# Grouping the small attention products of a hybrid decoder step, and loading the decode cache two steps at a time

## The chip, the core and the metric

The kernel runs on one core of one Trainium2 chip. The metric is the device time of one launch in microseconds, lower is better. The five engines that the text speaks of are PE (TensorE, matrix products; PEld are its weight loads), DVE (VectorE), ACT (ScalarE), POOL (GpSimd, which issues the indirect gathers) and SP (SyncE, which issues nearly all other transfers in one queue, in order).

## The reference, cut to what matters

One inference step of one decoder layer, for 1024 prompt tokens and for 8 decode sequences of 4 new tokens each:

```
proj = x @ w_in                                   # q,k,v of attention; q,k,v of GLA; gates
for g, (window, dil) in enumerate(((128,1),(512,4),(2048,16))):
    o_g, lse_g = dilated windowed softmax attention, 8 heads of 64, T5 bias
o_a  = sum_g softmax_g(lse_g) * o_g
o_b  = GLA recurrence (4 heads, 128 x 256 state), RMS norm, silu gate
x    = LN(ALPHA*x + (sigmoid(ga)*(o_a@wa) + sigmoid(gb)*(o_b@wb)) @ w_out)
x    = LN(ALPHA*x + PEER(x))                      # 8 heads x 16 of 16384 experts per token
```

In decode attention a new token at step s of its sequence (s = 0 to 3) reads, in groups 1 and 2, the cached keys at positions s, s+dil, s+2*dil and so on. The four steps of a sequence read four different key tiles of 128 positions, and four different value tiles. In group 0 (dilation 1) the four steps share one tile.

PEER picks experts per token and needs the rows of two 16384 x 1024 tables: for 544 columns of expert numbers (four blocks of 128 prompt tokens, and the decode tokens) the kernel gathers rows by index; for the other 512 tokens it multiplies by the whole tables ("dense").

## The kernel before, in words

The work is written as a program of tiles, and a scheduler puts the instructions of each engine into one fixed order before the launch: it follows the tiles' dependences, a priority (mostly the order in which the program text issues the work) and the time at which it expects an instruction's inputs and its tile's buffer to be free. On the chip every engine works through its own order without overtaking, and SP through its queue of transfers. A change of a few lines can therefore move instructions everywhere.

A tile's buffer comes from a ring named by a tag: `wst` (3 buffers, weight tiles as they land), `tq` (6 buffers of 2 KB per partition), `gr` (4 buffers of 4 KB per partition, made for the gathered rows), `pb` (3 PSUM banks), `ps` (4 PSUM banks).

The stages, on the time axis of the trace:

- `phase_a(0)`, from the start to about 918 us: projections of prompt tokens 0 to 511 and the 32 decode tokens (every weight tile lands in `wst`, is split into two parts by ACT, L143, and by DVE, L158, and is used by three products per output tile, L185 to L187), with three lanes that feed smaller work in between: prompt attention (`attend`), the GLA heads, and the decode lane (`sample_attention`, then `sample_gla`). It ends with the output projection and a layer norm, whose result is transposed (L815) for what follows.
- `query(0)`: the expert queries, first for token block 0 alone (32 weight tiles from `wq`, three products each), then for blocks 1 to 3. Its scores give the first top-k, and with it the first gather (L1233 on POOL, about 1065 us).
- `phase_a(1)` and its queries, for tokens 512 to 1023, to about 2300 us, with the gathers of the first blocks beside it (POOL issues, DVE multiplies and accumulates: L1239, L1272).
- `peer_dense`, to the end, with the last gathers beside it.

The small products of the change:

- `attend`, L356: for two query blocks p2 (and, where there are keys before them, two key blocks c) and the two heads r of a pair, one product of 64 rows. Head r uses rows 64r to 64r+63 of the array and writes to PSUM tile `p_[r]`.
- `sample_attention`, L1075 (keys): per sequence and group, for four head pairs hp and four steps s, a product that writes 32 output partitions 32s to 32s+31, that is, it uses 32 of the 128 columns of the array. Step s needs key tile `kts[s]`, one 256 KB transfer (L1068) into a `tq` buffer.
- `sample_attention`, L1128 (values): per sequence and group, four products of 32 columns, one per step, on value tiles loaded by L1125 into `tq`. L1120 is group 0's value product, L1132 what follows a sequence's value products.
- `sample_gla`, L1182 and L1187: the decode GLA's small products, on states that L1180 loads and L1191 stores.

One of these float32 products shows as two instructions in the trace (x2), so sixteen key products show as x32.

Of the kernel before, what the change touches and what calls it, by code (L numbers as in the profile page):

```python
# [3 lines left out]

# [1 line left out]

# [15 lines left out]
P = 128  # L22
# [59 lines left out]
def tile_hybrid_step(ctx, tc, I, O, dbg=None):  # L82
# [239 lines left out]
    def attend(b, g, hp, q, k, vP, ot, stat):  # L322

        bias = tb([P, 2, 256])
        nc.sync.dma_start(bias, biasd[g][:, 2 * hp:2 * hp + 2])
        np_ = 0 if b == 0 else 1 if g == 0 else 4
        if np_:
            pk, pv = tb([P, 4, P]), tb([P, 4, P])
            nc.sync.dma_start(pk[:, :np_], kprev[g][:, hp, :np_ * P].rearrange("d (p i) -> d p i", i=P))
            nc.sync.dma_start(pv[:, :np_], vprev[g][:, :np_, hp * P:(hp + 1) * P])  # L330

        def keys(p, c):
            if c:
                return k[:, p * P:(p + 1) * P]
            if g == 0 and p > 0:
                return k[:, (p - 1) * P:p * P]
            return pk[:, p] if np_ else None

        def values(p, c):
            if c:  # L340
                return vP[:, p, hp * P:(hp + 1) * P]
            if g == 0 and p > 0:
                return vP[:, p - 1, hp * P:(hp + 1) * P]
            return pv[:, p]

        po = pb()
        for pp in range(2):
            p_ = [pb([P, 2, 256]) for _ in range(2)]
            j0 = []
            for p2 in range(2):  # L350
                p = 2 * pp + p2
                j0.append(0 if keys(p, 0) is not None else P)
                for c in range(j0[p2] // P, 2):
                    for r in range(2):
                        rows = slice(64 * r, 64 * r + 64)
                        nc.tensor.matmul(p_[r][:, p2, c * P:(c + 1) * P], q[rows, p * P:(p + 1) * P], keys(p, c)[rows], start=True, stop=True)  # L356
            s2 = []
            parts = [(0, 2)] if j0[0] == j0[1] else [(0, 1), (1, 2)]
            for r in range(2):
                h = 2 * hp + r  # L360
                s_ = tb([P, 2, 256])
                s2.append(s_)
                for a, e in parts:
                    j = j0[a]
                    if F_TTR:
                        for p2 in range(a, e):
                            V.tensor_tensor_reduce(s_[:, p2, j:], p_[r][:, p2, j:], bias[:, r, j:], 1.0, -3e38, ALU.add, ALU.max, stat[:, 2 * pp + p2, h:h + 1])
                    else:
                        V.tensor_add(s_[:, a:e, j:], p_[r][:, a:e, j:], bias[:, r, None, j:].to_broadcast([P, e - a, 256 - j]))
                        V.reduce_max(stat[:, 2 * pp + a:2 * pp + e, h], s_[:, a:e, j:], axis=AX.X, negate=True)  # L370
                if F_TTR:
                    V.tensor_scalar(stat[:, 2 * pp:2 * pp + 2, h], stat[:, 2 * pp:2 * pp + 2, h], -1.0, None, ALU.mult)
                for p2 in range(2):
                    p, j = 2 * pp + p2, j0[p2]
                    nc.scalar.activation(s_[:, p2, j:], s_[:, p2, j:], AF.Exp, bias=stat[:, p, h:h + 1], accum_out=stat[:, p, 32 + h:33 + h])
            yield
            for p2 in range(2):
                p, c0 = 2 * pp + p2, j0[p2] // P
                t_ = pb([P, 2, 2, P])
                for r in range(2):  # L380
                    for c in range(c0, 2):
                        nc.tensor.transpose(t_[:, r, c], s2[r][:, p2, c * P:(c + 1) * P], ident)
                pt = tb([P, 2, 2, P])
                copy_any(pt[:, :, c0:], t_[:, :, c0:])
                for c in range(c0, 2):
                    v_ = values(p, c)
                    for r in range(2):
                        nc.tensor.matmul(po[r * 64:r * 64 + 64, p * P:(p + 1) * P], v_[:, r * 64:(r + 1) * 64], pt[:, r, c],
                                         start=c == c0, stop=c == 1)
                if p2 == 0:  # L390
                    yield

        cp = copy_act if F_OT and busy[0] else V.tensor_copy
        if g == 0:
            cp(ot[:, hp, :T], po)
        else:
            cp(ot[:, hp, :T].rearrange("d (i r) -> d r i", r=4), po.rearrange("d (r i) -> d r i", r=4))
# [639 lines left out]
        out.extend((f_(ef[0]), f_(ef[1]), ei, f_(gate)))  # L1037

    def sample_attention():
        for hf in range(2):  # L1040
            st = sb([P, 16], "s_st", 2)
            pr = tq([P, 3, 160])
            for g in range(3):
# [18 lines left out]
                for b4 in range(4):  # L1062
                    yield
                    b = hf * 4 + b4
                    kts = []
                    for s in range(1 if g == 0 else 4):
                        kt = tq([P, 4, P])
                        nc.sync.dma_start(kt, I["kc0"][b] if g == 0 else I[f"kc{g}"][b, s])  # L1068
                        kts.append(kt)
                    for hp in range(4):  # L1070
                        if g == 0:
                            nc.tensor.matmul(p_[:, b4], qf[:, hp], kts[0][:, hp], start=hp == 0, stop=hp == 3)
                            continue
                        for s in range(4):
                            nc.tensor.matmul(p_[32 * s:32 * s + 32, b4], qf[:, hp, 32 * s:32 * s + 32], kts[s][:, hp], start=hp == 0, stop=hp == 3)  # L1075
                w_ = pr[:, g]
                V.tensor_copy(w_, pn)
                for b4 in range(4):
# [35 lines left out]
            for b4 in range(4):  # L1114
                yield
                b = hf * 4 + b4
                p_ = pb()
                vt = tq([P, 512])
                nc.sync.dma_start(vt, I["cache1"][b, :, 1])
                nc.tensor.matmul(p_, tT[:, 0], vt, start=True, stop=False)  # L1120
                for g in (1, 2):
                    vts = []
                    for s in range(4):
                        vt = tq([P, 512])
                        nc.sync.dma_start(vt, I[f"cache{g + 1}"][b].rearrange("(i r) c d -> r i c d", r=DIL[g])[s, :, 1])  # L1125
                        vts.append(vt)
                    for s in range(4):
                        nc.tensor.matmul(p_[32 * s:32 * s + 32], tT[:, g, 32 * s:32 * s + 32], vts[s], start=False, stop=g == 2)  # L1128
                om = tq([P, 512])
                V.tensor_mul(om, p_, hm)  # L1130
                for hp in range(4):
                    nc.tensor.matmul(po[:, hp, 4 * b4:4 * b4 + 4], om[:, hp * P:(hp + 1) * P], sel[:, b4], start=False, stop=b4 == 3 and hp == 3)  # L1132
# [573 lines left out]
```

## Time and profile before

| what | us |
|---|---|
| three timed runs: median (lowest to highest) | 4177.53 (4170.21 to 4186.6) |
| the profiled execution: its time | 4168.93 |
| its span | 4167.2 |
| PE busy | 3739.9 (90%) |
| DVE busy | 3147.9 (76%) |
| POOL busy | 1345.5 (32%) |

The profiled execution is 8.6 us under the median of the timed runs. A sum made from the trace is a difference against 4168.93, and is carried over to the median as it is. Busy PE time overlaps from one matmul to the next (their ends are modelled), so the cost of a product is read from the start of one instruction to the start of the next.

### The profile page before, as it was taken

The numbers are of one execution on the slowest core, as the hardware profiler recorded it, in microseconds if no ns is written. First come the engines' busy times: TensorE is split into PE (matmuls) and PEld (weight loads), VectorE is DVE, ScalarE is ACT, GpSimd is POOL, SyncE is SP. The second block draws the span as 40 slices with busy tenths as digits, with TensorE's granted clock in tenths as the row PEclk, the third lists the DMA queues.
The fourth block names the chain that finished last, engine by engine and source line by source line (L and its number), as shares of the span: only waits on it lengthen the run. The fifth ranks groups of instructions, "written<-read, shape, count | busy, mean of one in ns | idle before, by whom it ended". The sixth has DMA issues, their size and how long they took to land.

```text
span 4167.2 us, 55732 instructions
## 1 busy us (share of the span) xinstructions
PE 3739.9 (90%) x18338; PEld 2890.6 (69%) x18338; DVE 3147.9 (76%) x7279; ACT 1444.7 (35%) x2958; POOL 1345.5 (32%) x1163
## 2 busy tenths in 40 slices
PE   8999999999897589999879866788999999999996
PEld 7888666665686478756757544677777777777775
DVE  2334433547999888788989998897888888888878
ACT  3334322324543354523225344332222233223323
POOL 0000000000245334354444322444444444444443
PEclk9999899999898689889889998999999999999997
DMA  8666465788688779778988756877998899999996
GB/s 276 199 215 201 164 201 184 262 272 277 200 310 299 226 260 327 255 243 304 317 300 283 222 199 241 274 249 269 312 311 310 309 318 311 318 318 320 312 320 248
DMA packets 455160, 1118.18 MB, mean 268 GB/s; under 512 B 48484, under 2 KB 133748, under 8 KB 444486
## 3 DMA queue, kind: packets, MB, share of 16 engines
q0 software_dynamic: 156672, 570.49, 39.8%
q1 hardware_dynamic: 298198, 544.13, 39.1%
q8 instruction: 144, 2.36, 0.2%
q14 instruction: 146, 1.20, 0.1%
HBM read 1043.94 MB, written 158.37 MB: 289 GB/s over the span
## 4 chain that ended last, share of the span: by engine, by line
PE 42%; DMA 20%; DVE 17%; issue 13%; POOL 5%; ACT 3%; SPq 0%; POOLq 0%; DVEq 0%; ACTq 0%
PE ps L185 9%; PE ps L186 9%; PE ps L187 9%; DMA gr<-pv,tkei 5%; DMA pg<-Gd 4%; POOL gr L1233 4%; DMA gr<-pu,tkei 3%; DVE gr L1239 3%; DMA wst<-pv 2%; DVE acc L1272 2%; DMA wst<-uT 2%; DVE wl L158 2%; PE pc L1312 2%; POOL gr L1254 2%; DVE tb L1309 1%
## 5 line engine op out<-in xcount | busy, mean ns | idle before, releaser
L1254 POOL DMA_INDIRECT gr<-pv,tkei x544 | 675.2, 1241 | 910.2 <-DVE acc L1272 567.3
L1233 POOL DMA_INDIRECT gr<-pu,tkei x544 | 651.1, 1197 | 951.3 <-DVE gr L1239 543.5
L185 PE MATMUL ps<-pg,wh 128*128 128x512 f32 (+3 forms) x2488 | 896.7, 362 | 65.7 <-ACT wh L143 43.5
L186 PE MATMUL ps<-pg,wl 128*128 128x512 f32 (+3 forms) x2488 | 896.0, 360 | 8.8 <-DVE wl L158 8.6
L187 PE MATMUL ps<-pg,wh 128*128 128x512 f32 (+3 forms) x2488 | 892.5, 360 | 0.0
L143 ACT ACTIVATE wh<-wst 128x512 fp32r<-128x512 f32 x740 | 462.2, 628 | 1148.7 <-DMA wst<-uT 347.7
L158 DVE TENSOR_TENSOR wl<-wst,wh 128x512 fp32r<-128x512 f32 x740 | 502.5, 683 | 346.1 <-ACT wh L143 317.2
L1239 DVE SCALAR_TENSOR_TENSOR gr<-gr,x1g 128x1024 f32<-128x1024 f32 x544 | 660.4, 1220 | 121.5 <-DMA gr<-pu,tkei 119.8
L1272 DVE SCALAR_TENSOR_TENSOR acc<-gr,act,acc 128x1024 f32<-128x1024 f32 x512 | 654.9, 1279 | 70.8 <-DMA gr<-pv,tkei 67.4
L185 PEld LDWEIGHTS ps<-pg,wh 128*128 128x128 f32 (+1 forms) x2488 | 472.2, 190 | 162.7 <-ACT wh L143 49.6
L186 PEld LDWEIGHTS ps<-pg,wl 128*128 128x128 f32 (+1 forms) x2488 | 472.9, 190 | 91.1 <-DVE wl L158 13.3
L187 PEld LDWEIGHTS ps<-pg,wh 128*128 128x128 f32 (+1 forms) x2488 | 472.5, 190 | 77.1 <-issue 10.7
L185 PE MATMUL ps<-wh,pg 128*128 128x512 f32 x832 | 342.2, 418 | 33.2 <-ACT wh L143 20.3
L186 PE MATMUL ps<-wh,pg 128*128 128x512 f32 x832 | 341.6, 411 | 3.7 <-DVE pg L158 3.7
L187 PE MATMUL ps<-wl,pg 128*128 128x512 f32 x832 | 323.5, 415 | 4.0 <-DVE wl L158 3.6
L143 ACT ACTIVATE pg<-wst 128x512 fp32r<-128x512 f32 x256 | 160.0, 630 | 448.0 <-DMA wst<-pv 428.8
L185 PEld LDWEIGHTS ps<-wh,pg 128*128 128x128 f32 x832 | 177.6, 214 | 90.3 <-ACT wh L143 26.7
L1046 POOL MEMSET tq<- 128x512 f32 x6 | 3.2, 526 | 661.7 <-issue 287.2
L187 PEld LDWEIGHTS ps<-wl,pg 128*128 128x128 f32 x832 | 174.9, 213 | 51.8 <-issue 10.8
L185 PE MATMUL ps<-tq,pg 128*128 128x512 f32 x512 | 203.4, 400 | 7.9 <-ACT t L1356 7.8
L186 PEld LDWEIGHTS ps<-wh,pg 128*128 128x128 f32 x832 | 177.4, 213 | 44.1 <-issue 10.5
L186 PE MATMUL ps<-tq,pg 128*128 128x512 f32 x512 | 202.4, 395 | 0.0
(421 smaller groups left out, 5728.0 us busy)
## 6 DMA issues: line engine op xcount, KB each, us to landing
o_old<-cache SPq DMA_DIRECT2D x256, 256.0 KB
wst<-uT SPq DMA_DIRECT2D x256, 256.0 KB
wst<-pv SPq DMA_DIRECT2D x256, 256.0 KB
wst<-wT SPq DMA_DIRECT2D x192, 256.0 KB
Gd<-pg SPq DMA_DIRECT2D x32, 1024.0 KB
pg<-Gd SPq DMA_DIRECT2D x32, 1024.0 KB
wst<-wN SPq DMA_DIRECT2D x112, 256.0 KB
wst<-wq SPq DMA_DIRECT2D x96, 256.0 KB
```

What stands on the lines that cost most here:

```text
L143: nc.scalar.activation(out, in_, AF.Copy, scale=scale)
L158: V.tensor_sub(lo, src, hi)
L185: nc.tensor.matmul(out, lh, rh, start=first, stop=False)
L186: nc.tensor.matmul(out, ll, rh, start=False, stop=False)
L187: nc.tensor.matmul(out, lh, rl, start=False, stop=last)
L1046: nc.gpsimd.memset(qf, 0.0)
L1233: nc.gpsimd.indirect_dma_start(out=u, out_offset=None, in_=I["pu"], in_offset=bass.IndirectOffsetOnAxis(ap=ei[:, j:j + 1], axis=0))
L1239: V.scalar_tensor_tensor(u, u, 1.0, x1, ALU.mult, ALU.mult, accum_out=act[:, j:j + 1])
L1254: nc.gpsimd.indirect_dma_start(out=u, out_offset=None, in_=I["pv"], in_offset=bass.IndirectOffsetOnAxis(ap=ei[:, j:j + 1], axis=0))
L1272: V.scalar_tensor_tensor(acc, u, act[:, j:j + 1], acc, ALU.mult, ALU.add, accum_out=None if j < n - 1 or decode else sums[:, 0, 0:1])
L1309: last.append(V.tensor_scalar(og[:, k], consts["rows"], eT[:, 1, n:n + 1], eT[:, 2, n:n + 1], ALU.is_equal, ALU.mult))
L1312: nc.tensor.matmul(p_[:, k], o1[:, k], og[:, k], start=True, stop=True)
```

## The change

Three edits. In `attend` the score products of a pair of query blocks are listed for all p2, c and r, with r = 1 before r = 0, and every product after the first carries an edge that keeps it behind the first on PE. In `sample_attention` a helper `two` loads the keys (or values) of two steps into one `gr` buffer, two transfers of 512 KB in place of four of 256 KB; and the sixteen key products, or four value products, run over s = 3, 2, 1, 0 with the same kind of edge behind the first, which needs the second transfer.

```
-                for c in range(j0[p2] // P, 2):
-                    for r in range(2):
-                        rows = slice(64 * r, 64 * r + 64)
-                        nc.tensor.matmul(p_[r][:, p2, c * P:(c + 1) * P], q[rows, p * P:(p + 1) * P], keys(p, c)[rows], start=True, stop=True)
+                pairs.extend((p2, p, c, r) for c in range(j0[p2] // P, 2) for r in (1, 0))
+
+            first = None
+            for p2, p, c, r in pairs:
+                rows = slice(64 * r, 64 * r + 64)
+                with tc.issue_after(first.ins) if first else nullcontext():
+                    mm = nc.tensor.matmul(p_[r][:, p2, c * P:(c + 1) * P], q[rows, p * P:(p + 1) * P], keys(p, c)[rows], start=True, stop=True)
+                first = first or mm
...
+        def two(src):
+            t = [sb([P, 2, 512], "gr", 4) for _ in range(2)]
+            for i in range(2):
+                nc.sync.dma_start(t[i], src(2 * i))
+            return lambda s: t[s // 2][:, s % 2]
...
-                    kts = []
-                    for s in range(1 if g == 0 else 4):
+                    if g == 0:
                         kt = tq([P, 4, P])
-                        nc.sync.dma_start(kt, I["kc0"][b] if g == 0 else I[f"kc{g}"][b, s])
-                        kts.append(kt)
+                        nc.sync.dma_start(kt, I["kc0"][b])
+                        for hp in range(4):
+                            nc.tensor.matmul(p_[:, b4], qf[:, hp], kt[:, hp], start=hp == 0, stop=hp == 3)
+                        continue
+                    kts = two(lambda s: I[f"kc{g}"][b, s:s + 2].rearrange("s p h k -> p s (h k)"))
+                    first = None
                     for hp in range(4):
-                        for s in range(4):
-                            nc.tensor.matmul(p_[32 * s:32 * s + 32, b4], qf[:, hp, 32 * s:32 * s + 32], kts[s][:, hp], start=hp == 0, stop=hp == 3)
+                        for s in (3, 2, 1, 0):
+                            with tc.issue_after(first.ins) if first else nullcontext():
+                                mm = nc.tensor.matmul(p_[32 * s:32 * s + 32, b4], qf[:, hp, 32 * s:32 * s + 32], kts(s)[:, hp * P:(hp + 1) * P], start=hp == 0, stop=hp == 3)
+                            first = first or mm
...
-                    for s in range(4):
-                        vt = tq([P, 512])
-                        nc.sync.dma_start(vt, I[f"cache{g + 1}"][b].rearrange("(i r) c d -> r i c d", r=DIL[g])[s, :, 1])
-                        vts.append(vt)
-                    for s in range(4):
-                        nc.tensor.matmul(p_[32 * s:32 * s + 32], tT[:, g, 32 * s:32 * s + 32], vts[s], start=False, stop=g == 2)
+                    vts = two(lambda s: I[f"cache{g + 1}"][b].rearrange("(i r) c d -> r i c d", r=DIL[g])[s:s + 2, :, 1].rearrange("r i d -> i r d"))
+                    first = None
+                    for s in (3, 2, 1, 0):
+                        with tc.issue_after(first.ins) if first else nullcontext():
+                            mm = nc.tensor.matmul(p_[32 * s:32 * s + 32], tT[:, g, 32 * s:32 * s + 32], vts(s), start=False, stop=g == 2)
+                        first = first or mm
```

The scheduler's order shows what became of this. First PE in decode attention, the values of one sequence in group 2 before (`tq` tiles are the loaded values, `pb` the PSUM tile, `ps` products are the projections; L1128):

```order
L1128 MATMUL pb_5404<-tq_5420,tq_5318 32x512
L185 MATMUL ps_5821<-pg_107,wh_5826 128x256
L186 MATMUL ps_5821<-pg_107,wl_5827 128x256
L187 MATMUL ps_5821<-pg_109,wh_5826 128x256
L185 MATMUL ps_5822<-pg_107,wh_5826 128x288
L186 MATMUL ps_5822<-pg_107,wl_5827 128x288
L187 MATMUL ps_5822<-pg_109,wh_5826 128x288
L185 MATMUL ps_5821<-pg_108,wh_5858 128x256
L186 MATMUL ps_5821<-pg_108,wl_5859 128x256
L187 MATMUL ps_5821<-pg_110,wh_5858 128x256
L185 MATMUL ps_5822<-pg_108,wh_5858 128x288
L1128 MATMUL pb_5404<-tq_5422,tq_5318 32x512
```

The same sequence's values of groups 1 and 2 in the changed order (now L1140; L1134 is group 0's product; `gr` buffers hold two steps each):

```order
L1134 MATMUL pb_5372<-tq_5373,tq_5286 128x512
L1140 MATMUL pb_5372<-gr_5377,tq_5286 32x512 x2
L1140 MATMUL pb_5372<-gr_5376,tq_5286 32x512 x2
L1140 MATMUL pb_5372<-gr_5385,tq_5286 32x512 x2
L1140 MATMUL pb_5372<-gr_5384,tq_5286 32x512 x2
L466 MATMUL pb_5398<-pg_4409,tb_5310 128x256
```

Products that stood alone between projections now stand as eight in a row. Over the whole order the 64 value products stood in 37 runs (26 of one, 4 of two, one of three, 4 of four, one of five, one of six) and stand in 10 (7 of eight, and one each of one, three and four); the 256 key products stood in 56 runs (35 of one, 5 of two, 15 of thirteen, one of sixteen) and stand in 21.

Second, PE in prompt attention, the last products of one pair of query blocks before (L356 writes the PSUM tiles `pb_161`, head 0, and `pb_162`, head 1; L388 is the preceding blocks' product with the values):

```order
L388 MATMUL pb_115_590<-tb_147_795,pg_16_143 64x128 x4
L356 MATMUL pb_161_885<-t2_128_679,t2_113_587 128x128 x3
L388 MATMUL pb_115_590<-tb_158_875,pg_16_143 64x128 x4
L356 MATMUL pb_162_886<-t2_128_679,t2_113_587 128x128 x3
L185 MATMUL ps_269_1525<-pg_4_107,wh_272_1530 128x256
```

And in the changed order (L359 in place of L356, L392 in place of L388):

```order
L392 MATMUL pb_115_590<-tb_147_795,pg_16_143 64x128 x4
L359 MATMUL pb_162_886<-t2_128_679,t2_113_587 128x128 x3
L392 MATMUL pb_115_590<-tb_158_875,pg_16_143 64x128 x4
L359 MATMUL pb_161_885<-t2_128_679,t2_113_587 128x128 x3
L185 MATMUL ps_269_1525<-pg_4_107,wh_272_1530 128x256
```

The two heads have changed places and stand as far apart as before. Over the whole order the 312 products stood in 80 runs and stand in 81; of the runs, 21 held both heads (129 products), and 23 do now (138 products).

Third, SP in the first query stage before (`wst` tiles are its weights from `wq`; `tb` tiles the decode GLA states, loaded by L1180 and stored by L1191):

```order
L172 DMA wst_8998<-wq 128x512
L1191 DMA o_st_s<-tb_8289 128x2x256
L172 DMA wst_9007<-wq 128x512
L172 DMA wst_9039<-wq 128x512
L1180 DMA tb_8502<-state 128x2x256
L1191 DMA o_st_s<-tb_8377 128x2x256
L1180 DMA tb_8503<-state 128x2x256
L172 DMA wst_9068<-wq 128x512
```

The same queue in the changed order, from the seventh of these weight tiles on:

```order
L1204 DMA o_st_s<-tb_8630 128x2x256
L172 DMA wst_8764<-wq 128x512
L172 DMA wst_8796<-wq 128x512
L172 DMA wst_8825<-wq 128x512
L172 DMA wst_8834<-wq 128x512
L172 DMA wst_8843<-wq 128x512
```

The decode GLA's transfers have left this stage: the decode lane is through earlier, and its GLA stands before the layer norm's transposes, about half of its products before the last projection of `phase_a(0)` and half behind it. The last 21 of the 64 value products stood behind that last projection, and now all stand ahead of it, with two of the group 0 products (L1120) and three of the sets that end a sequence (L1132).

## Rows read from the trace of the kernel before

**Rows 1.** Page: busy tenths of PE and DVE in 40 equal slices of the span.

```profile
PE   8999999999897589999879866788999999999996
DVE  2334433547999888788989998897888888888878
```

**Rows 2.** Stretches: PE, PEld, DVE, ACT, POOL busy us (instructions), clock, DMA share, GB/s.

```profile
0.00:918.00 918.00, 895.29 (x5458) 686.31 (x5458) 361.33 (x851) 282.46 (x679) 17.35 (x66) 0.98 0.66 218
918.00:944.00 26.00, 21.30 (x92) 9.02 (x91) 17.57 (x32) 10.77 (x22) 0.22 (x2) 0.87 0.92 319
944.00:1008.00 64.00, 60.61 (x286) 34.41 (x286) 42.47 (x135) 28.51 (x67) 0.00 (x0) 0.95 0.75 239
1065.00:4130.00 3065.00, 2702.70 (x12262) 2115.48 (x12261) 2646.73 (x5944) 1075.61 (x2069) 1325.47 (x1093) 0.93 0.84 285
```

**Rows 3.** Order of time on PE, key products: start us, us, instructions.

```profile
462.85 1.08 PE L1075 MATMUL pb<-tq,tq 128*32 128x128 f32 x32
...
480.49 0.28 PE L186 MATMUL ps<-pg,wl 128*128 128x256 f32 x1
480.61 0.27 PE L187 MATMUL ps<-pg,wh 128*128 128x256 f32 x1
480.81 0.41 PE L1075 MATMUL pb<-tq,tq 128*32 128x128 f32 x2
...
481.39 0.30 PE L186 MATMUL ps<-pg,wl 128*128 128x288 f32 x1
```

**Rows 4.** Order of time on PE, value products: four together, then one.

```profile
579.73 1.02 PE L1120 MATMUL pb<-tq,tq 128*128 128x512 f32 x2
580.68 1.07 PE L1128 MATMUL pb<-tq,tq 128*32 128x512 f32 x8
581.67 0.70 PE L462 MATMUL pb<-pg,tb 128*128 128x256 f32 x2
...
585.33 0.30 PE L187 MATMUL ps<-pg,wh 128*128 128x288 f32 x1
585.56 1.05 PE L1128 MATMUL pb<-tq,tq 128*32 128x512 f32 x2
586.53 0.39 PE L185 MATMUL ps<-pg,wh 128*128 128x256 f32 x1
586.76 0.28 PE L186 MATMUL ps<-pg,wl 128*128 128x256 f32 x1
```

**Rows 5.** Order of time on PE, prompt scores: one head's four products; six of both.

```profile
155.14 1.16 PE L356 MATMUL pb<-t,t 64*128 64x128 f32 x8
...
169.36 0.94 PE L356 MATMUL pb<-t,t 64*128 64x128 f32 x12
```

**Rows 6.** Groups by line and form, PE, 918 to 1065 us: busy, mean ns, idle.

```profile
L1187 PE MATMUL pb<-pg,tb 32*128 32x256 f32 x64 | 18.9, 418 | 0.0
L1128 PE MATMUL pb<-tq,tq 128*32 128x512 f32 x42 | 14.4, 701 | 2.4 <-DMA tq<-cache 2.4
L1182 PE MATMUL pb<-tb,pg 128*32 128x256 f32 x64 | 8.9, 402 | 1.9 <-DMA tb<-state 1.8
```

**Rows 7.** Order of time on DVE: the layer norm's last step.

```profile
927.98 4.87 DVE L972 SCALAR_TENSOR_TENSOR pg<-pg,nw,pg 128x1024 f32<-128x1024 f32 x4
```

**Rows 8.** What PE waited for before L1075, and before L1128 (us, times).

```profile
  DMA tq<-kc: 4.2, 4
...
  DMA tq<-cache: 7.9, 7
```

**Rows 9.** Waits, 944 to 1012 us: us in total, times, longest.

```profile
ACT wh L143 <- DMA wst<-wq: 16.6, 11, 3.5
```

**Rows 10.** Order of time on SP in that stage.

```profile
962.83 0.33 SPq L172 DMA_DIRECT2D wst<-wq  x1
...
965.60 0.33 SPq L172 DMA_DIRECT2D wst<-wq  x1
```

**Rows 11.** Order of time on POOL: the first gather, and what it waited for.

```profile
1065.24 1.11 POOL L1233 DMA_INDIRECT gr<-pu,tkei  x1 [139.42 <-DVE pg L927]
```

More of the change, by code (lines that the diff above doesn't have):

```diff
@@ L2 @@
 from collections import deque
-from contextlib import ExitStack
+from contextlib import ExitStack, nullcontext
 import numpy as np
@@ L348, in attend @@
             p_ = [pb([P, 2, 256]) for _ in range(2)]
-            j0 = []
+            j0, pairs = [], []
             for p2 in range(2):
@@ L1064, in sample_attention @@
                     b = hf * 4 + b4
-                    kts = []
-                    for s in range(1 if g == 0 else 4):
+                    if g == 0:
                         kt = tq([P, 4, P])
-                        nc.sync.dma_start(kt, I["kc0"][b] if g == 0 else I[f"kc{g}"][b, s])
-                        kts.append(kt)
-                    for hp in range(4):
-                        if g == 0:
-                            nc.tensor.matmul(p_[:, b4], qf[:, hp], kts[0][:, hp], start=hp == 0, stop=hp == 3)
-                            continue
-                        for s in range(4):
-                            nc.tensor.matmul(p_[32 * s:32 * s + 32, b4], qf[:, hp, 32 * s:32 * s + 32], kts[s][:, hp], start=hp == 0, stop=hp == 3)
+                        nc.sync.dma_start(kt, I["kc0"][b])
[4 more added lines that the diff above has]
+                    first = None
+                    for hp in range(4):
+                        for s in (3, 2, 1, 0):
+                            with tc.issue_after(first.ins) if first else nullcontext():
+                                mm = nc.tensor.matmul(p_[32 * s:32 * s + 32, b4], qf[:, hp, 32 * s:32 * s + 32], kts(s)[:, hp * P:(hp + 1) * P], start=hp == 0, stop=hp == 3)
+                            first = first or mm
                 w_ = pr[:, g]
@@ L1121, in sample_attention @@
                 for g in (1, 2):
-                    vts = []
-                    for s in range(4):
-                        vt = tq([P, 512])
-                        nc.sync.dma_start(vt, I[f"cache{g + 1}"][b].rearrange("(i r) c d -> r i c d", r=DIL[g])[s, :, 1])
-                        vts.append(vt)
-                    for s in range(4):
-                        nc.tensor.matmul(p_[32 * s:32 * s + 32], tT[:, g, 32 * s:32 * s + 32], vts[s], start=False, stop=g == 2)
+                    vts = two(lambda s: I[f"cache{g + 1}"][b].rearrange("(i r) c d -> r i c d", r=DIL[g])[s:s + 2, :, 1].rearrange("r i d -> i r d"))
[4 more added lines that the diff above has]
+                        first = first or mm
                 om = tq([P, 512])
```

## The prediction

> **What bounds the kernel now.** I read the page's slices first: PE is at nine tenths nearly throughout, DVE at two to five tenths for about the first ten slices and at eight or nine from the twelfth on [rows 1]. Then the stretches, for sums: to 918 us PE is busy 895.29 us of 918 and DVE only 361.33, so `phase_a(0)` is bound by PE, and an instruction taken off PE there brings everything behind it forward. From the first gather (1065 us) to 4130 us PE is busy 2702.70 and DVE 2646.73 us of 3065: both are near full, and the gathers run beside both to the end [rows 2]. The change has no instruction there but prompt attention of the second half. Third, the order of time on PE around the touched products, for their prices; last, the waits and SP's queue in the stage from 944 to 1008 us.
>
> **Key products of the decode lane.** One product alone costs PE 0.53 us: from the start of the projection before it (480.61) to that of the second projection behind it (481.39) are 0.78 us, less two projections of about 0.125 us (0.12 from 480.49 to 480.61, with 256 columns; the next has 288); both neighbours start late [rows 3]. Sixteen products in a row took at most 1.08 us, since four of 32 columns each run at once [rows 3]; with 0.2 us for the late neighbours that is 1.2. Before: 35 x 0.53 + 5 pairs at 0.6 + 16 long runs at 1.2 = 41 us. In the changed order 256 products stand in 21 runs: 16 x 1.0 + 21 x 0.2 = 20 us. The term is -21.
>
> **Value products.** One alone: 585.33 to 586.76 is 1.43 us, less two projections of 0.13 = 1.17. Four together: 580.68 to 581.67 = 0.99, as long as one alone (585.56 to 586.53 = 0.97) [rows 4]. The Trainium skill, TensorE: Matmul & The Clock Gate, section Part 3, gives 3.07 times for four row tiles and 2.38 for three column tiles; the row has 3.9 times for four column tiles. By the page a group of four would take 1.3 lone products in place of 1.0, and the sixteen groups 5 us more in all; the row decides here.
>
> Before 918 us stand 43 of the 64 in the order before: 23 alone, 2 pairs, 4 fours: 23 x 1.17 + 6 x 1.2 = 34 us. In the changed order all 64 stand there: 7 runs of eight at 2 x 0.99 + 0.2 = 2.2, three short ones at 1.2: 19 us. The term is -15. With them come two products of L1120 at 0.95 and three sets of L1132, 8 short instructions each, taken at the same price: 5 x 0.95 = +5 [rows 4].
>
> **What the faster lane pulls forward.** The decode GLA follows in the lane. Its two lines, L1187 and L1182, took 18.9 and 8.9 us of PE, with 64 instructions each, behind the layer norm [rows 6]. Half of that now stands ahead of the last projection of `phase_a(0)`: 14 us, and 2 for its late neighbours: +16. The other half falls into the layer norm's gap.
>
> **New waits.** A group's first product now needs the second of two 512 KB loads, and what waits behind it on PE are the projections. The `gr` ring holds two groups, so that in two places, where two groups stand back to back, four loads (2 MB) start together, with the next group some 15 projections later. PE waited 4.2 us for key tiles and 7.9 for value tiles before, all of it in few places [rows 8]. Ends for the extra: 0, and 1 MB at the 239 GB/s of the query stage [rows 2], 4.4 us, for a dozen groups, 50 us. I take 5, near the low end: the loads of the other groups are issued a group ahead, where `tq` let only part of one stand ahead. Sum ahead of the layer norm: -21 - 15 + 5 + 16 + 5 = -10.
>
> **The layer norm's gap.** It lasted from 918 to 944 us, and its last vector step ended at 932.85 [rows 7]; then 12 us went into transposes that shared PE with value products. Those are gone, GLA products take part of the place, and they stand ahead of the transposes with 2 MB of state loads of their own. Between -8 (the transposes alone, 4 us) and +8 (the states land late). I take -2.
>
> **The first query stage.** PE was busy for 60.61 of its 64 us, but 28 of these were the decode GLA's [rows 2, 6]; what is left, 33 us, does not fill the time that the 32 weight tiles took to come, 2.0 us each, and ACT waited 16.6 us for their landings [rows 9]. Between the weight loads SP served state loads and stores, each waiting for a buffer. These have left, the weight loads stand in one row. Where three loads followed each other at the shortest spacing, SP issued them 1.4 us apart [rows 10]. Ends: 2.0 (nothing gained) and 1.4 (-19 us). I take 1.6, nearer the row with little in between, since DVE's other work also delays the release of a `wst` buffer: 32 x 0.4 = -13.
>
> **Prompt attention.** Its edge does not group the two heads: each half waits for its own PSUM buffer, and head 1 now takes the one that comes first. The trace has the price of this: four products of one head take 1.16 us, six of both heads 0.94 [rows 5], so pairing would be worth about 0.9 us per pair of query blocks. The order has 81 runs in place of 80, and 9 more of the 312 products in runs of both heads: 9 x 0.1, under 1 us, taken as 0. If the flip delays head 0's softmax, DVE has room before 918 us [rows 2]; in the second half of the prompt it has none, and I let that go into the range.
>
> **The sum.** -10 - 2 - 13 = -25 us at the first gather, 1065.24 in the trace [rows 11]. Behind it the work is the same; from the 560th gather multiply on, the order on DVE has at most five weight splits more or fewer ahead of each, of 1180, so PE's and DVE's shares of the end are dealt as before. In the middle (up to the 560th) the difference is up to 24 splits, in both directions, which is what can eat or add some 15 us. 4168.93 - 25 = 4144; carried to the median, 4177.53 - 25 = 4152.
>
> **Rivals.**
> All PE savings arrive: the GLA does not cost what it pulls forward, because in the query stage PE was then the limit (busy 60.61 of 64 us [rows 2]) and its 28 us count in full. Then every product counts, the value products from 918 us on too (42 instructions, 14.4 us [rows 6]): -21 for the keys, 19 - 34 - 14 = -29 for the values, +5 for new waits, -45 together: 4132. Against it: what those 14.4 us stood in was the layer norm's gap, where PE waits for DVE and ACT anyway.
> The gain is absorbed: gathers start 25 us sooner, but the middle of the kernel is reordered, DVE and PE are both near full there, and the pairing of the two is worse by as much. 4165 to 4180. For it: DVE at 8 and 9 tenths from the twelfth slice [rows 1], and the 24 splits. Against it: a pure shift needs nothing from DVE.
> Slower: the groups wait for their pairs of loads. 32 groups, each held until 1 MB has landed. With 4.4 us per load and half of it uncovered, 32 x 2.2 = 70 us, against 25: 4222. It decides from 0.8 us a group on (25 / 32) and is slower by 0.5% from 1.45 us. For it: PE is in order and has nothing to put in the place; weight loads queue on SP behind the 2 MB. Against it: 12 us of such waits in 93 runs of the two kinds [rows 8].
> That the change doesn't do what it says is so for prompt attention, and is part of the forecast.
>
> **How the numbers follow.** Half a per cent, 21 us, is about what a measurement of this kernel can tell from no change; faster is below 4156.6. The forecast has 0.52: centred on 4152 with a spread of about 12 us from the ends above (own range 4136 to 4168), 0.34 of it faster and 0.18 the same. All savings arrive: 0.17, all faster. Absorbed: 0.20, 0.02 of it faster and 0.18 the same. Slower: 0.11, all slower. Together faster 0.53, the same 0.36, slower 0.11. The range leaves out about a tenth on each side: 4124 to 4188.
>
> **What would show it.** In the changed profile: runs of x32 key products near 1.05 us and runs of x16 value products near 2 us; PE's wait for `gr` tiles under 10 us in all; the last projection of `phase_a(0)` at about 908 us in place of 918; weight tiles of the first query stage about 1.6 us apart; the first gather at about 1040. The forecast is wrong if the first gather comes after 1060, or if it comes at 1040 and the end does not follow; waits for `gr` over 30 us would make it the slower rival.

## The result: slower by 0.6%, where 0.6% faster was forecast

| | median us (runs) | ratio to the kernel before | 95% interval |
|---|---|---|---|
| before | 4176.85 (5) | | |
| changed | 4206.41 (5) | 1.0060 | 1.0030 to 1.0089 |

The changed kernel lies outside the range. Its profiled execution took 4206.41 us, its span 4204.4. The page's slices of the changed kernel, PE, DVE and granted clock:

```profile
PE   8999999998797698789879867789999999999996
DVE  3333533557999888887988897887888888888877
PEclk9999799999997599878889989899999999999998
```

Beside [rows 1] PE falls from 9 to 7 tenths in the seventeenth slice (1682 to 1787 us), where the clock goes to 8 and then 7 tenths. The same stretches as in [rows 2], of the changed kernel:

```profile
0.00:918.00 918.00, 888.35 (x5579) 698.23 (x5579) 362.95 (x870) 279.48 (x674) 16.19 (x66) 0.95 0.68 227
...
944.00:1008.00 64.00, 51.84 (x197) 34.48 (x197) 46.42 (x169) 37.15 (x87) 0.00 (x0) 0.87 0.72 229
1065.00:4130.00 3065.00, 2657.32 (x12028) 2079.63 (x12027) 2607.66 (x5887) 1057.11 (x2019) 1302.95 (x1074) 0.91 0.82 280
```

From 1065 us on PE is busy 45 us less and does 234 instructions less in the same time: it waits more. Where it waits, a count of products in the traces shows. Every kernel here runs the same 13,344 projection products (L185 to L187) in the same stages, so the start of the projection that has n others ahead of it, less its start in the kernel before, is the delay at that place. For the changed kernel and for six of the kernels that follow (us):

| n | start before | place | changed | heads_flip | heads_softmax_flip | change_softmax_flip | decode_alone | decode_loads | slices_flip |
|---|---|---|---|---|---|---|---|---|---|
| 1300 | 277.8 | first half's attention | +12.7 | +8.1 | +3.4 | +6.8 | +2.4 | +7.2 | +3.8 |
| 3660 | 915.2 | last of `phase_a(0)` | +10.2 | +12.6 | +21.5 | -9.2 | -2.8 | -9.3 | -32.7 |
| 3800 | 1027.5 | end of first query stage | -17.7 | +9.6 | +23.0 | -37.5 | -32.0 | -32.7 | -25.4 |
| 5460 | 1783.3 | just ahead of second `mix` | -21.3 | +16.6 | -2.8 | -45.1 | -45.8 | -44.9 | -46.6 |
| 5485 | 1831.2 | just behind it | +12.0 | +53.4 | -3.3 | -39.7 | -44.2 | -42.5 | -44.8 |
| 9000 | 3044.1 | dense stage | +20.0 | +53.7 | +2.3 | -16.2 | -29.2 | -34.5 | -44.3 |
| 13300 | 4116.2 | 51 us ahead of the end | +40.4 | +71.0 | +15.0 | -13.1 | -15.0 | -25.1 | -31.3 |

(The last row is not a difference of medians. The profiled execution of the kernel before was 8 us faster than its median, and slices_flip, 31 us ahead there, is 18 us ahead at the end of its span.) The changed kernel was 21 us ahead and lost 33 us between the 5460th and the 5485th projection. What it waited for there, from 1740 to 1840 us (us in total, times, longest):

```profile
PE pb L438 <- DVE tb L430: 24.7, 1, 24.7
```

L438 is the second half's `mix`, L430 its last step on DVE ahead of that product. The stretch from 1740 to 1860 us, first in the changed kernel, then in the one before (columns as in [rows 2]):

```profile
1740.00:1860.00 120.00, 85.03 (x307) 51.65 (x306) 105.91 (x166) 24.93 (x52) 62.09 (x51) 0.72 0.77 255
```

```profile
1740.00:1860.00 120.00, 114.41 (x417) 75.46 (x416) 108.68 (x160) 33.42 (x70) 62.30 (x43) 0.83 0.75 245
```

DVE is equally busy in both, PE 29 us less in the changed kernel. From 1766 to 1839 us the granted clock of the changed kernel is 0.53, nearly all at 1.2 GHz, but that is not where the 33 us come from, since the kernel before has half clock at this place too. Here is the time from the 5460th to the 5485th projection alone, first in the changed kernel, then in the one before:

```profile
1762.00:1843.20 81.20, 46.23 (x120) 22.40 (x119) 73.33 (x113) 12.82 (x25) 42.37 (x33) 0.58 0.69 225
```

```profile
1783.30:1831.20 47.90, 44.31 (x92) 22.22 (x91) 44.29 (x58) 7.98 (x17) 29.27 (x19) 0.57 0.73 233
```

PE is busy 46.2 us and 44.3, at a clock of 0.58 and 0.57, and idle 35.0 us and 3.6. So the loss is waiting: 24.7 us for L430, and the rest in short waits of 1 to 5 us around it, where no projections are left to fill them. Behind this place the changed kernel loses 28 us more by the last row of the table, and the other six 13 to 29 us; that is not explained here.

What the prediction asked of the touched products is there. Order of time on PE in the changed kernel, key products (L1088) and value products (L1140), for [rows 3, 4]:

```profile
490.29 1.94 PE L1088 MATMUL pb<-gr,tq 128*32 128x128 f32 x32
...
509.29 1.08 PE L1088 MATMUL pb<-gr,tq 128*32 128x128 f32 x32
...
587.62 1.92 PE L1140 MATMUL pb<-gr,tq 128*32 128x512 f32 x16
```

What PE waited for before L1088, the key tiles, and before L1140, where no value tile is among it (for [rows 8]); then the wait of ACT for weight tiles from 953 to 1000 us, the first query stage (9.5 us where [rows 9] has 16.6); SP's queue in it (for [rows 10]); and the first gather (for [rows 11]):

```profile
  DMA gr<-kc: 7.0, 4
...
  DMA o_old<-cache: 1.1, 2
```

```profile
ACT wh L143 <- DMA wst<-wq: 9.5, 11, 3.2
```

```profile
968.40 8.68 SPq L172 DMA_DIRECT2D wst<-wq  x6
```

```profile
1052.47 1.60 POOL L1246 DMA_INDIRECT gr<-pu,tkei  x1 [114.27 <-PE ps L186]
```

### The profile page after: what moved, and what is told of

It is laid out like the page before. It is cut to its first block, busy times and chain, and to the rows that moved or that the text cites. A ratio compares the mean times of both kernels' runs of the same rounds, so it can differ in the third digit from the quotient of the medians.

```text
span 4204.4 us, 55583 instructions
## 1 busy us (share of the span) xinstructions
PE 3720.0 (88%) x18338; PEld 2903.6 (69%) x18338; DVE 3145.5 (75%) x7279; ACT 1446.1 (34%) x2958; POOL 1345.1 (32%) x1163
## 4 chain that ended last, share of the span: by engine, by line
issue 16%; DMA 13%; DVE 10%; POOL 7%; PE 6%; ACT 1%; POOLq 0%; SPq 0%; DVEq 0%; ACTq 0%
DMA gr<-pv,tkei 7%; POOL gr L1246 5%; DVE acc L1285 2%; POOL gr L1267 2%; DMA gr<-pu,tkei 1%; DVE tb L1322 1%; PE ps L185 1%; DMA pg<-Gd 1%; DMA wst<-uT 1%; PE ps L186 1%; PE ps L187 1%; DMA wst<-pv 1%; DVE tb L1319 1%; DVE wl L158 1%; DVE pg L158 1%
## 5 line engine op out<-in xcount | busy, mean ns | idle before, releaser
L185 PE MATMUL ps<-pg,wh 128*128 128x512 f32 (+3 forms) x2488 | 905.1, 366 | 85.9 <-ACT wh L143 49.7
L186 PE MATMUL ps<-pg,wl 128*128 128x512 f32 (+3 forms) x2488 | 906.2, 365 | 14.6 <-DVE wl L158 13.6
L187 PE MATMUL ps<-pg,wh 128*128 128x512 f32 (+3 forms) x2488 | 899.7, 362 | 0.0
L185 PEld LDWEIGHTS ps<-pg,wh 128*128 128x128 f32 (+1 forms) x2488 | 480.2, 193 | 184.6 <-ACT wh L143 55.5
L187 PEld LDWEIGHTS ps<-pg,wh 128*128 128x128 f32 (+1 forms) x2488 | 480.3, 193 | 78.0 <-issue 11.6
L185 PE MATMUL ps<-wh,pg 128*128 128x512 f32 x832 | 339.8, 415 | 31.9 <-ACT wh L143 22.1
L187 PE MATMUL ps<-wl,pg 128*128 128x512 f32 x832 | 319.4, 409 | 7.4 <-DVE wl L158 7.4
L185 PEld LDWEIGHTS ps<-wh,pg 128*128 128x128 f32 x832 | 175.9, 212 | 84.9 <-ACT wh L143 29.8
L185 PE MATMUL ps<-tq,pg 128*128 128x512 f32 x512 | 199.3, 397 | 10.5 <-ACT t L1369 10.4
L187 PEld LDWEIGHTS ps<-wl,pg 128*128 128x128 f32 x832 | 172.1, 210 | 48.3 <-DVE wl L158 15.7
L158 DVE TENSOR_TENSOR pg<-wst,pg 128x512 fp32r<-128x512 f32 x256 | 174.5, 688 | 34.5 <-ACT pg L143 30.6
```

Source lines behind the costliest of these rows:

```text
L158: V.tensor_sub(lo, src, hi)
L185: nc.tensor.matmul(out, lh, rh, start=first, stop=False)
L186: nc.tensor.matmul(out, ll, rh, start=False, stop=False)
L187: nc.tensor.matmul(out, lh, rl, start=False, stop=last)
```

## The experiments

Theory 1: prompt attention's flip (head 1's scores ahead of head 0's) makes the second half's attention end late, so that its `mix` finds no other work left for PE; the decode part gains what was forecast. Theory 2: the decode part costs the time. Theory 3: any new order moves the end by some 25 us. The built orders sharpen the first. With and without the edges (`issue_after`) the order of PE, DVE, ACT and SP is the same row for row, in prompt attention and in the decode lane: the edges move nothing. What moves instructions is the flip of the heads, the flip of the slices and the loads of two steps. And the order already holds the loss: counted in projections of the whole kernel, the second half's last score product stands at 5280 before and at 5418 in the changed kernel, while `mix` begins on PE at 5472 in both. DVE's minimum, the first step of that `mix`'s chain (L415, in the changed kernel L419), stands behind 405 weight splits before and behind 416 after, with none left; the chain's last step (L426, L430) behind 414 and 416.

**Parts alone.** Each against the kernel before:

```
heads_flip      L354  - for r in range(2):          + for r in (1, 0):
decode_alone    the change's hunks in sample_attention, attend as before
decode_loads    as decode_alone, without edges, slices s from 0 to 3
slices_flip     L1074, L1127  - for s in range(4):  + for s in (3, 2, 1, 0):
```

(heads_flip also turned the loop of the same words at L1048, copies on POOL; the order of the other four engines is that of the attention edit alone.)

> The kernel before with one edit: in prompt attention the score products of head 1 are issued ahead of those of head 0; decode as before. (With the edges of the change added, the order of every engine is this one, row for row.) Theory 1, the flip costs the time: in the built order the last score product of the second half stands 134 projections later than before (5414 against 5280), and the minimum of `mix` on DVE behind 416 weight splits in place of 405, so that nothing is left to stand between them and PE waits there. Of the change's own loss, 13 us lie in the first half's attention and some 45 between 1770 and 1840 us: about 4225 us (4205 to 4240). Theory 2, the decode lane's part costs it: within 8 us of before, 4170 to 4186. Theory 3, any new order moves the end by some 25 us in either direction: anywhere from 4150 to 4205, with nothing to be seen at the second `mix`.

> The change in the decode lane alone (loads of two steps, slices from 3 to 0, edges), prompt attention as before. Theory 1: it keeps what the changed kernel had gained up to the last gathers ahead of the second `mix`, 26 to 32 us, and loses nothing behind it, since `mix` stands at 406 splits: 4150 us (4135 to 4165), with PE's wait at the second `mix` under 8 us. Theory 2: about 4205 us. Theory 3: anywhere from 4150 to 4205.

> The loads of two steps alone: no edges, slices in their old order 0 to 3, prompt attention as before. The built order has 26 runs of key products where the decode part has 20, and else nearly the same. Theory 1: 4152 us, within 6 us of the decode part alone. Theory 2, if it is the row buffers that hold things up: 4205 us; if it is the order of slices: 4177 us. Theory 3: anywhere from 4150 to 4205.

> The kernel before with one edit: the four slices of a step's key and value products are issued from 3 to 0; one load of 256 KB a slice and everything else as before. In the built order that alone puts the 256 key products into 15 runs (before 56) and the 64 value products into 15 runs of four or eight (before 37): the first product needs the last tile, so the rest can follow at once. Theory 1: the products' own gain without the gain in the first query stage, where the loads stand as before: keys -21, values -15, decode GLA pulled ahead as far as the lane now runs, +8: 4150 us (4140 to 4165). Theory 2, if the order of slices were what costs: 4205 us. Theory 3: anywhere from 4150 to 4205.

| | median us | ratio | 95% interval |
|---|---|---|---|
| heads_flip | 4235.54 | 1.0140 | 1.0118 to 1.0161 |
| decode_alone | 4158.17 | 0.9949 | 0.9930 to 0.9968 |
| decode_loads | 4137.87 | 0.9919 | 0.9899 to 0.9938 |
| slices_flip | 4155.41 | 0.9948 | 0.9929 to 0.9966 |

Theory 1 holds and theory 2 falls: the flip alone costs 1.4% and the decode part gains 0.5%, 0.9% together, where the change measured 0.6% (0.3 to 0.9). The table of delays parts the flip's price in the change, the changed kernel against decode_alone: 13 us at the 3660th projection, 25 at the 5460th, 56 at the 5485th, 55 at the 13,300th. Theory 3 doesn't give the largest part, since 32 us come at one place, though orders do scatter: decode_loads and decode_alone end 20 us apart. PE's wait at the second `mix` in heads_flip, and the first gather in decode_loads, which was forecast for 1040:

```profile
PE pb L434 <- DVE tb L426: 27.6, 1, 27.6
```

```profile
1037.45 1.60 POOL L1242 DMA_INDIRECT gr<-pu,tkei  x1 [116.60 <-PE ps L186]
```

slices_flip groups as well without any new load: the first product then needs the tile that lands last, and the rest follow at once (15 runs of key products in the built order, 56 before). Its price is waiting: 16.9 us for key tiles and 16.1 for value tiles, where PE waited 4.2 and 7.9 before [rows 8] and 7.0 and none in the changed kernel with its larger loads. That decode_loads has a median 20 us under decode_alone's was not expected and stays open (the two intervals just meet); at the 6000th projection decode_alone is still 10 us ahead.

**Why the flip delays attention.** Order of time on PE and then on DVE for one pair of heads in the second half, in the kernel before: head 0's four products, its two reductions, head 1's four products, its reductions.

```profile
1613.66 0.49 PE L356 MATMUL pb<-tb,t 64*128 64x128 f32 x2
...
1622.21 0.49 PE L356 MATMUL pb<-tb,t 64*128 64x128 f32 x2
```

```profile
1617.36 0.42 DVE L367 CUSTOM_DVE_ANT_0 tb<-pb,tb 128x256 f32<-128x256 f32 x1
...
1624.54 0.41 DVE L367 CUSTOM_DVE_ANT_0 tb<-pb,tb 128x256 f32<-128x256 f32 x1
```

And one in the changed kernel: head 1's products, head 0's, then all four reductions in a row.

```profile
1610.22 0.48 PE L359 MATMUL pb<-tb,t 64*128 64x128 f32 x2
...
1646.22 0.49 PE L359 MATMUL pb<-tb,t 64*128 64x128 f32 x2
```

```profile
1650.85 0.40 DVE L371 CUSTOM_DVE_ANT_0 tb<-pb,tb 128x256 f32<-128x256 f32 x1
...
1651.88 0.41 DVE L371 CUSTOM_DVE_ANT_0 tb<-pb,tb 128x256 f32<-128x256 f32 x1
```

Head 1's PSUM tile was filled at 1611 and read from 1651.5. This is the longest of the second half's 24 groups: 36 us between the first products of the two heads, the next 20, the median 2 (before also 2, the longest 8.5). In heads_flip the same two groups have 45 and 18 us, in heads_softmax_flip below none has over 9.2. The softmax loop still takes head 0 first, so the tile that is filled first is let go last, and a pair needs two `pb` banks at once where one after the other would do. (That the three banks of the ring are the link is read from the order; a larger ring was not tried.) In the changed kernel 23 of the second half's 24 groups have all eight records of their reductions in one row on DVE; in the kernel before 5 have, and in heads_softmax_flip 5 again. If that is the cause, flipping the softmax loop too must undo it:

```
              - s2 = []                       + s2 = [None, None]
L359 (L363)   - for r in range(2):            + for r in (1, 0):
              -     s2.append(s_)             +     s2[r] = s_
```

heads_softmax_flip has this on heads_flip, change_softmax_flip on the changed kernel.

> The kernel before with two edits in prompt attention: head 1's score products ahead of head 0's, and the softmax loop behind them in the same order, head 1 first. Theory 1, the flip costs because DVE still reduces head 0 first, so that the PSUM buffer that is filled first is let go last and the attention chain of the second half ends 134 projections later: with both flipped the built order has the last score product at 5280 and the minimum of the second `mix` behind 405 splits, as before, so the time is that of before, 4176 us (4165 to 4187), and PE waits under 5 us at the second `mix`. Rival, the flipped products themselves cost (they pair worse on PE, or meet other loads): 4235 us, as with the products alone flipped.

> The changed kernel with one edit more: the softmax loop of prompt attention takes head 1 first too. Theory 1: the loss at the second `mix` goes and the decode lane's gain stays; the built order has the last score product at 5318 (5418 in the changed kernel, 5280 in the one before) and the minimum behind 408 splits (416, 405): 4158 us (4145 to 4172). Rival, the loss of the changed kernel comes from both parts together: between 4185 and 4206 us.

heads_softmax_flip: 4181.41 us, ratio 1.0005 (0.9988 to 1.0023); change_softmax_flip: 4167.74, 0.9977 (0.9963 to 0.9991). One loop's order takes 1.4% away from the one and 0.8% from the other. The stretch of the second `mix` in heads_softmax_flip, and the longest wait of PE there:

```profile
1740.00:1860.00 120.00, 112.66 (x416) 74.30 (x415) 107.68 (x148) 30.64 (x63) 49.54 (x43) 0.84 0.75 244
```

```profile
PE pb L434 <- issue: 3.3, 1, 3.3
```

The rival, that the flipped products themselves cost, falls. PE's idle time just ahead of the second `mix` follows the number of splits that stand ahead of the minimum: 1.5 to 3.3 us behind 405 or 406 splits (before, heads_softmax_flip, decode_alone), 8.9 and 10.3 behind 408 (heads_flip_first, change_softmax_flip), 24.7 to 27.6 behind 416 (changed, heads_flip, heads_flip_second). In the first half the reversal does not show: heads_softmax_flip is 21.5 us behind at the 3660th projection, more than heads_flip, and makes it up by the 5460th. change_softmax_flip reached the 5485th projection 40 us ahead and ended some 10 us later than expected (the kernel before, at 4181.3 beside it, 5 us); by the 9000th it had lost 24 of the 40, where no instruction of the change stands, and that is not explained.

**One half at a time.** `for r in (1, 0)` in the first half only, and in the second only:

> The kernel before with head 1's score products ahead of head 0's in the first half of the prompt alone. In the built order the last score product of the first half stands at 2026 projections (1972 before), that of the second half at 5319 (5280), and the minimum of the second `mix` behind 408 splits (405; 416 with both halves flipped). Theory 1 with the losses adding up: 12 us in the first half, as with both halves flipped, and a quarter of the 43 at the second `mix`: 4197 us (4185 to 4208). Rival, the first half's 12 us are absorbed in the layer norm's gap or the middle: 4178 us.

> The kernel before with head 1's score products ahead of head 0's in the second half of the prompt alone: last score product at 5409 projections (5280), minimum of the second `mix` behind 416 splits, with no split left (405). Theory 1: all of the loss at the second `mix` and none ahead of it: 4176 + 43 = 4219 us (4208 to 4230), PE's wait there 20 us or more. Rival, the end of the second half's attention matters only together with the later first half: 4176 to 4190 us.

heads_flip_first: 4199.93, 1.0045 (1.0027 to 1.0063), as expected in the number, but not by the sum expected: in its trace 11.9 us are lost by the 3660th projection, as forecast, then made up in the middle, as the rival had it (-4.0 at the 5460th); 5 go at the second `mix` and 13 behind it, where nothing was changed. heads_flip_second: 4205.12, 1.0062 (1.0039 to 1.0085), 14 us less than expected; its trace loses 35 us at the second `mix` (from -8.2 to +26.6), with PE waiting

```profile
PE pb L434 <- DVE tb L426: 26.2, 1, 26.2
```

So the second half alone makes the long wait. The miss is in what lies ahead of it: 8 us that another order happened to win.

**Does an earlier end of attention, or another place of the decode GLA, win more?** One number each: `ATTR` (0.7, 0.65) to (0.7, 0.9) on slices_flip, to (0.7, 0.8) on decode_loads; `DECRATE` 0.35 to 0.45 and to 0.30 on decode_loads.

> The kernel with the slices from 3 to 0 (one load of 256 KB a slice) and one number changed: the rate of the second half's attention lane 0.9 in place of 0.65. In the built order the minimum of the second `mix` comes behind 398 weight splits in place of 405, and its first product ahead of 63 projections where before none were left. Theory 1, what the end of attention costs is the PE time that is left uncovered at the second `mix`, and there is some of it in the kernel before too (41 us at the half clock from 1788 us on): 10 to 15 us less than with the slices alone, 4143 us (4130 to 4156). Rival, attention that is brought forward only pushes the projections back: 4155 us.

> The kernel with the loads of two steps alone, and the rate of the second half's attention lane 0.8 in place of 0.65: the minimum of the second `mix` behind 400 splits (405), its first product ahead of 20 projections (none). Theory 1: 5 to 10 us less than with the loads alone, 4130 us (4120 to 4138). Rival: 4138 us.

> The kernel with the loads of two steps alone, and the decode lane's rate 0.45 in place of 0.35: all 82 rows of the decode GLA stand ahead of the last projection of `phase_a(0)`, where 44 stood, and none in the layer norm's gap. Theory 1, the GLA costs PE its time wherever PE is busy, and only what lies in the layer norm's gap is hidden: the 14 us that were hidden there come on top, 4150 us (4142 to 4160). Rival, nothing is hidden in that gap, because its products delay the transposes by as much: 4138 us.

> The kernel with the loads of two steps alone, and the decode lane's rate 0.30 in place of 0.35: 78 of the 82 rows of the decode GLA stand in the first query stage, as in the kernel before (74), none ahead of the last projection of `phase_a(0)` (44). Theory 1, state loads between the weight loads hold the query stage up by some 20 us, which the GLA's 14 us saved ahead of it do not make good: 4146 us (4138 to 4156). Rival, what the GLA costs in the two places is equal: 4138 us.

| | median us | ratio | 95% interval |
|---|---|---|---|
| slices_flip_rate90 | 4170.94 | 0.9984 | 0.9964 to 1.0003 |
| decode_loads_rate80 | 4160.81 | 0.9953 | 0.9934 to 0.9971 |
| decode_loads_rate45 | 4159.52 | 0.9946 | 0.9925 to 0.9967 |
| decode_loads_rate30 | 4139.56 | 0.9907 | 0.9884 to 0.9929 |

The two attention rates went wrong: both kernels reach the 5485th projection where their partners do (-45.5 beside -44.8, and -43.7 beside -42.5), so attention that is pulled ahead pushes the projections back by as much, as the rival had it. Both then end 0.3 to 0.4% later than their partners; a part of that is a wait at the next layer norm, in slices_flip_rate90 and then in slices_flip, from 2060 to 2420 us:

```profile
PE ps L815 <- DVE pg L972: 36.2, 1, 36.2
```

```profile
PE ps L815 <- DVE pg L972: 24.5, 1, 24.5
```

decode_loads_rate45 ended at the upper edge of its range, for another reason than the one given: with the whole GLA ahead of the layer norm it stood 4 us ahead of decode_loads at the 3980th projection, so nothing came on top there; it fell back in the dense stage. In decode_loads_rate30 the rival held: with the GLA in the query stage the 3660th projection comes 16 us sooner than in decode_loads and the 3980th 1 us later, so the GLA costs PE the same in either place. decode_loads and decode_loads_rate30 beat both kernels, by 0.8% and 0.9% of the time before.

## Why the prediction was wrong, step by step

- **Keys -21, values -15: the prices were right.** slices_flip shows them by themselves, since its GLA stays behind the layer norm; but it leaves 24 of the 64 value products behind the last projection of `phase_a(0)`, so that by the prediction's prices its terms are -22 (15 runs of key products) and -22 (ten runs of four values). Up to that projection, before and in slices_flip:

```profile
0.00:915.20 915.20, 892.49 (x5446) 684.24 (x5447) 359.73 (x847) 280.35 (x673) 17.35 (x66) 0.98 0.66 218
```

```profile
0.00:882.50 882.50, 849.25 (x5440) 680.42 (x5441) 358.11 (x847) 279.67 (x673) 17.12 (x66) 0.97 0.69 225
```

PE is busy 43 us less, for 44 by the prices, and idle 10.5 us more, which leaves the 32.7.
- **Decode GLA pulled ahead, +16: right.** 92 of its instructions stand ahead of that projection in the changed kernel and take 13 us from start to start.
- **New waits, +5: wrong sign.** PE waited 7.0 us for `gr` tiles, 4 times, where it had waited 4.2 and 7.9 for `tq` tiles [rows 8]. The slower rival, groups that wait for their loads, falls, though the kernel is slower.
- **Sum of -10 there: not held by the changed kernel (+10.2).** Three kernels have the change's decode part, and the same number of PE instructions (5608 or 5609) ahead of this projection: the changed one, decode_alone (-2.8) and change_softmax_flip (-9.2). In this order:

```profile
0.00:925.40 925.40, 895.75 (x5609) 702.88 (x5610) 368.11 (x880) 281.18 (x678) 16.19 (x66) 0.95 0.67 226
```

```profile
0.00:912.40 912.40, 887.38 (x5608) 699.55 (x5609) 370.75 (x880) 281.70 (x678) 15.91 (x66) 0.97 0.68 230
```

```profile
0.00:906.10 906.10, 875.30 (x5609) 692.45 (x5610) 371.16 (x879) 281.66 (x678) 15.95 (x66) 0.98 0.69 231
```

They are idle 30, 25 and 31 us, but PE is busy for 896, 887 and 875 us, at a granted clock of 0.95, 0.97 and 0.98. So the 20 us between the ends are not a wait; they go with more time at half clock, of which the last section shows the longest piece. What sets that time was not tried. That -10 came out in change_softmax_flip, and in decode_loads (-9.3), is in part luck, as the waits had the wrong sign and decode_alone has -2.8.
- **Layer norm's gap -2: right; query stage -13: sign right, size short.** In the changed kernel the gap is 2.5 us shorter, and the query stage gains 25 us from there to the 3800th projection. SP issued six weight tiles in 8.68 us, 1.45 each, near the end of 1.4 that the bounds had [rows 10]. From the first product of the 32 tiles to the first one behind them are 49 us, 1.5 a tile, near the 1.6 taken; but in the kernel before they are 73 us, 2.3 a tile, and not the 2.0 that the term began from.
- **"Prompt attention ... taken as 0": the step that failed.** It counted what the flip does to runs of products on PE (81 in place of 80) and let a delayed softmax "go into the range". It did not ask who reads the tile that is now filled first. That reader's loop was left as it was, and the price of the flip is 55 us in the trace of the changed kernel, against decode_alone's, and 1.4%, some 58 us, in heads_flip. Of it, 32 to 37 us come at the second `mix`, and these are shown to be the order of reading, since all but 5 go when the softmax loop is turned too. The 13 us ahead of the 3660th projection are not: turning the softmax loop takes 19 us off the changed kernel there and adds 9 to heads_flip.
- **"Behind it the work is the same": failed with it.** The end was carried from the first gather, with the second half's different order taken for a scatter of 15 us. The order that was at hand had it: DVE's minimum of the second `mix` behind the last of 416 splits, so nothing was left to cover the wait. The scatter was put too low as well: decode_alone is 44 us ahead behind that `mix` and 15 at the 13,300th projection. The forecast named as its refutation a first gather after 1060, or one at 1040 and an end that doesn't follow. It was 1052, between the two, and the end did not follow.
- **Rivals.** "Absorbed in the middle" had the right place and too small a price, since it asked only for the gain to be eaten, not for a wait on top.

## What to carry to other kernels

Flip the order in which tiles are filled only together with the order in which they are read; otherwise the first one filled holds its buffer until the last one comes, and with a ring of three buffers that lengthened the whole chain here. To make small products stand together, let the first of them need the input that lands last; that alone did it here, while explicit edges moved nothing. When a change reorders a kernel, look at each place where a stage ends and one engine's chain is all that is left, and see how many instructions still stand beside it.

## What the hardware showed unexpectedly

The granted clock fell to half without any idle time on PE that the profile shows. In the changed kernel, from 469.7 to 507.2 us, and just behind it (columns as in [rows 2]):

```profile
469.70:507.20 37.50, 37.50 (x177) 21.20 (x178) 13.03 (x21) 1.89 (x3) 0.00 (x0) 0.50 0.33 108
507.20:530.00 22.80, 22.80 (x266) 19.70 (x263) 8.49 (x23) 6.22 (x14) 0.00 (x0) 1.00 0.89 313
```

PE was busy for all of the 37.50 us at 1.2 GHz (0.50); the run of sixteen key products in it took 1.94 us in place of 1.08. Just before the fall stood, among others, products of few rows, the bias products with 41 of 128 and `mix` with 8:

```profile
467.06 0.48 PE L1069 MATMUL pb<-tq,relS 41*32 41x160 f32 x8
...
468.47 1.12 PE L438 MATMUL pb<-tb,tb 8*128 8x512 f32 x2
```

More products of `mix` with 8 rows stand in the stretch, up to 501 us. The second `mix` has the same in the kernel before, from 1788 to 1829 us, with PE busy for 38.78 of 40.90 us:

```profile
1788.30:1829.20 40.90, 38.78 (x72) 18.70 (x71) 37.58 (x49) 5.56 (x12) 23.49 (x16) 0.50 0.74 235
```

The Trainium skill, TensorE: Matmul & The Clock Gate, Part 1, ties the fall to PE being idle; these rows, with PE busy throughout or nearly so, don't agree. Which of these products brings it about was not tried.
